# Third and fourth mLSTM output gates and two tiles of the first merge gate as seven-product pairs

## The chip, the cores and the metric

The kernel runs on one core of one Trainium2 chip. The metric is the device time of one execution in microseconds; lower is better. The core has a matrix engine (TensorE, PE in the profile, with its weight loads as PEld), a vector engine (VectorE, DVE), an activation engine (ScalarE, ACT), GpSimd (POOL) and SyncE (SP). The last two and ACT also issue DMAs. Matrix products are summed in eight PSUM banks; everything else lies in SBUF or in DRAM.

## What is computed

Two layers of a hybrid encoder block on one sequence of 512 frames, model width 1024, in float32. What matters of the reference:

```python
h = rmsnorm(x, norm1_g[i])
z = h @ w_in[i] + b_in[i]
_, _, mv, mo, mi, mf, rq, rk, rv, rg, gm, gr = split_cols(z)
...
hm = mlstm_chunkwise(q, k, v, log_i, log_f)          # 4 heads, dk = dv = 256
y_m = sigmoid(mo) * head_layernorm(hm, m_norm_g[i], M_HEADS)
...
merged = sigmoid(gm) * (y_m @ w_bm[i]) + sigmoid(gr) * (y_r @ w_br[i])
x = x + merged @ w_out[i]
```

`mo` (1024 columns, 256 per head) are the output gates of the four mLSTM heads, `gm` (1024 columns) is the first merge gate. The change concerns how the columns of `mo` for the third and fourth head, and columns 256 to 511 of `gm`, are multiplied out.

## The kernel before

**Precision.** Each float32 operand is split into a high part that the matrix engine takes as it is and a low part that is the remainder (`split`, L320: one ACT copy, one DVE subtraction). A product is three matmuls, high by high, high by low and low by high (`mm3`, L501).

**Units.** All weights pass through a written-out list of units (`unit_list`, L172), consumed in order. A `T8` unit (`t8`, L506) is one 1024 x 128 tile of weights against all 512 frames: 8 row blocks of 3 matmuls with 512 columns, 24 in all. A `V` unit is a quarter of a value projection. A `PAIR` unit (`run_pair`, L538) is two neighbouring tiles, 256 columns of weights, done as a 2 x 2 block product by a seven-product scheme: the weights are cut into four blocks (B11 to B22), the frames into two halves and the rows of x into even and odd tiles, and seven products P1 to P7 of half the size take the place of eight. Each is 4 x 3 matmuls with 256 columns, 84 in all. A `WIDE` unit is the same scheme on 1024 columns of weights.

**What a pair needs besides.** Sums of weight blocks: t1 and t3 are made once in DRAM by accumulating DMAs on GpSimd's queue (`step`, L372, L379); t2 and t4 are formed on DVE when the pieces are prepared (L481, L484). A pair has four pieces: A is B11 and t1, C is B22 and t3, B is B21 and t2, D is t4 (L97). Sums of the operand: `xs_sums(k)` (L1264) adds the high and low part of two tiles of the normed x, forms four combinations of their halves and splits them again, k = 0 to 3 for the eight tiles. The products P5, P6, P3 and P7 read these sums; P1, P2 and P4 read x itself. `pair_tiles` (L618) gathers the seven results into two 128 x 512 outputs: four ACT copies, three DVE additions, each of 256 columns, and calls `consume` when P4 has been added. P4 is put off: it is issued when the next unit, or the next scores or attention, calls `flush` (L529). One of the two outputs comes with its sign turned, which `SIGN` (L62) undoes.

**Preparation.** Raw pieces are loaded by SyncE's queue in the order of use into four buffers, and a fifth while there is room (`fill_raws`, L415), and split into three shared buffers and one for D (`prep_next`, L445), for single tiles two units ahead (`LOOK`), for pairs by the table `READY` (L122). The load of a block sum waits for its DMAs.

**Pace of the sums.** Each unit adds to a credit what the constants say of its time and its loads (`tick`, L387): a share (`SHARE` until the unit of layer 0's third retention gate, `LATER` from there) of 5.45 us for a tile less 1.5 for its load, 9.9 and 3.9 for a pair. At credit 0 or more the next sum step goes out (`pace`, L383) and takes off `STEP`. The steps run over the groups in the order of `groups()` (L148), layer 0 first, and each waits for the matmul last issued. A load asserts that the steps of its block were issued.

**Order of the work.** The build lays out each engine's instructions from priorities that follow the source order and from when it expects their operands; `ahead()` raises the priority of the evictions of pairs. So the order on an engine can differ from the source's.

**The mLSTM stage (L1331 to L1384).** In layer 0 it lasts from about 7 to 284 us. Head by head: projections q and k (four `T8`) with a causal convolution on DVE; `m_scores(h)`, the decayed score matrix; `m_attend(h)`, the numerators, whose head norm (`head_stats`, `head_scale` L880) runs on DVE with a power on GpSimd; `m_gates(h)`, two `T8` with a sigmoid on ACT; `m_back(h)`, eight transposes of the scaled numerators, multiplied by the gates on DVE. Two value projections lie in between (`mv_vals`). `xn_tile(k)` makes the normed x. Until all eight are there, the products run on the un-normed operand `xa`, and their results are multiplied by the norm on DVE (L894). The first four tiles of `gm` are `T8` units as well (`gm_tile`, L1249): two ahead of the scores of head 0, the third between the gates and the transposes of head 0, the fourth between the gates and the transposes of head 2. They are spilled to DRAM on ACT's queue and read back for the merge (`bm_tile`, L1391). The last four tiles of `gm` are pairs already (`gm_gates`, L1241). The stage ends with `rv_vals(0)`, the first `WIDE` unit.

Of the kernel before, what the change touches and what calls it, by code (L numbers as in the profile page):

```python
# [108 lines left out]
HALVES = [(WIDE[x][0], u) for x, u in TURNS]  # L109

SOON = ("w_in", 0, CGM + 2 * P)
STEP, SHARE, LATER = 1.13, 0.75, 0.75
TIME = {"PAIR": (9.9, 3.9), "WIDE": (5.45, 2.7), "FULL": (9.9, 5.0)}


# [32 lines left out]
def groups():  # L148


    g = {}
    for i in range(L):
        def rqk(h):
            return [("w_in", 0, c + k * 256) for k in (h, h + 1) for c in (CRQ, CRK)]

        g[i, "rv0"] = [("w_in", 0, CRV)]
        g[i, "rqk0"] = rqk(0)
        g[i, "gm"] = [("w_in", 0, CGM + 256 * p) for p in (2, 3)]
        g[i, "rw0"] = [("w_in", 0, CRG)]
        g[i, "rv2"] = [("w_in", 0, CRV + 1024)]  # L160
        g[i, "rqk2"] = rqk(2)
        g[i, "rw2"] = [("w_in", 0, CRG + 1024)]
        g[i, "gr"] = [("w_in", 0, CGR + 256 * p) for p in range(4)]
        for b in range(4):
            f = [p for c, p in FPAIRS[i] if c == b]
            if f:
                g[i, f"fp{b}"] = [("w_ff1", 0, b * 1024 + 256 * p) for p in f]
            g[i, f"ff{b}"] = [("w_ff2", b * 1024, 256 * p) for p in range(4)]
    return g


def unit_list(i):  # L172
# [19 lines left out]
    def mo(h):  # L192
        for d in range(2):
            t8("w_in", CO + h * 256 + d * P)
# [5 lines left out]
    def full(w, col=0, row=0, lo=0, hi=8):  # L200
        for c in range(lo, hi):
            t8(w, col + c * P, row)
# [3 lines left out]
    full("w_in", CGM, 0, 0, 2)  # L206
    mqk(1)
    mo(0)
    full("w_in", CGM, 0, 2, 3)
    mqk(2)  # L210
    mo(1)
    v(CV + 512)
    mqk(3)
    mo(2)
    full("w_in", CGM, 0, 3, 4)
    mo(3)
    u.append(("WIDE", (i, "rv0"), 0))
    full("w_bm", 0, 0, 0, 4)
    rqk(0)
# [34 lines left out]
def build(ctx, tc, ins, out):  # L254
# [755 lines left out]
    for i in range(L):  # L1010
# [125 lines left out]
        def m_gates(h, act, nrm):  # L1136
            return [gated(f"l{i}m{h}o{v}", t8(act, f"l{i}m{h}o{v}"), nrm, AF.Sigmoid, bcol(i, "bo", 2 * h + v))
                    for v in range(2)]

        def m_back(h, gs, num):  # L1140
            gate_out(f"l{i}m{h}o", gs, num, [bcol(i, "gmn", 2 * h + v) for v in range(2)], ym, 2 * h)

# [98 lines left out]
        def gm_gates(p):  # L1241
            def consume(g):
                for d in range(2):
                    ac.activation(g[d], g[d], AF.Sigmoid, bias=bcol(i, "bgm", 2 * p + d), scale=SIGN[d])
                    gm[2 * p + d] = g[d]

            pair_tiles(f"l{i}bgm{p}", xs, consume)

        def gm_tile(c, act, nrm):  # L1249

            g = gated(f"l{i}bgm{c}", t8(act, f"l{i}bgm{c}"), nrm, AF.Sigmoid, bcol(i, "bgm", c))
            nc.scalar.dma_start(gm_dram[i, c], g)
# [5 lines left out]
        def xn_tile(k, x=x):  # L1258
            t = tmp(f"l{i}xnr{k}")
            ve.scalar_tensor_tensor(t, x[k], n1.col(k), n1.b, OP.mult, OP.mult)  # L1260
            xn[0][k] = bpool.tile([P, T], F32R, name=f"l{i}xnh{k}", tag="big", bufs=KT)
            split(t, xn[0][k], xn[1][k])
# [91 lines left out]
        qk = m_qk(1, xa, n1, xn_tile)  # L1354
        num = m_attend(0, pt, vv)
        gs = m_gates(0, xa, n1)
        xn_tile(4)
        gm_tile(2, xa, n1)
        for k in (5, 6, 7):
            xn_tile(k)  # L1360
        m_back(0, gs, num)
        xa_pool.release()
# [5 lines left out]
        xs_sums(0)  # L1368
        num = m_attend(1, pt, vv)
        gs = m_gates(1, xn, None)  # L1370
        vv = mv_vals(1, xn, None, lambda: m_back(1, gs, num))
        xs_sums(1)
        pt = m_scores(2, qk)
        qk = m_qk(3, xn, None)
        xs_sums(2)
        num = m_attend(2, pt, vv)
        gs = m_gates(2, xn, None)
        gm_tile(3, xn, None)
        m_back(2, gs, num)
        xs_sums(3)  # L1380
        pt = m_scores(3, qk)
        gs = m_gates(3, xn, None)
        num = m_attend(3, pt, vv)
        vv = rv_vals(0, lambda: m_back(3, gs, num))  # L1384

# [453 lines left out]
```

## Time and profile before

| | |
|---|---|
| median of 3 runs | 2285.81 us (2283.84 to 2286.82) |
| the profiled execution | 2280.56 us |
| its span, first to last instruction | 2278.8 us |
| TensorE busy | 2261.4 us, 99% of the span |
| VectorE busy | 1746.8 us, 77% |
| ScalarE busy | 1280.9 us, 56% |
| GpSimd busy | 605.8 us, 27% |
| moved by DMA | 499.32 MB |

Times in the trace are counted from the span's start. Names are the program's own with buffer numbers left out: `l0m2o` is layer 0, mLSTM head 2 (the third, counted from 0), output gate; `l0bgm` a single tile of the first merge gate, `l0bgm2` its pair 2 with the banks a, b and c behind the name; `l0m1s` head 1's scores, `l0m0ot` head 0's transposes, `l0m2z` head 2's projections, `l0xsl` the low part of the sums of normed x; `w` the split weights of a single tile, `w_A` to `w_D` those of a pair. A row of the view in order of time gives start, duration, engine, line, operation and operands, with the engine's idle time ahead of it and what ended that in square brackets; a matmul's duration includes the fill and drain, so the rate is read from one start to the next. A row of the grouped view ends with the count, the busy time, the mean duration in ns, and the idle time ahead. A row of the view by stretch gives its ends, its length and the busy time of each engine.

### The profile page before, as it was taken

How to read it: one execution, taken by the hardware profiler on the slowest of the kernel's cores; microseconds unless marked ns; L12 is line 12 of the kernel's file. 1: busy time of each engine (PE TensorE's matmuls, PEld its weight loads, DVE VectorE, ACT ScalarE, POOL GpSimd, SP SyncE). 2: the span in 40 equal slices, each digit the busy share in tenths (PEclk: the TensorE clock that was granted, in tenths of full speed). 3: DMA queues.
4: the chain of work that ended last, by engine and by line, in shares of the span. 5: the costliest groups of instructions: out<-in, count | busy, mean ns of one | idle time of the engine just before them, and what ended most of it. 6: DMA issues, size and time to landing. Idle time of an engine off the chain costs nothing.

```text
span 2278.8 us, 36395 instructions
## 1 busy us (share of the span) xinstructions
PE 2261.4 (99%) x13532; PEld 2007.0 (88%) x13532; DVE 1746.8 (77%) x2680; ACT 1280.9 (56%) x1881; POOL 605.8 (27%) x952
## 2 busy tenths in 40 slices
PE   9999999999999999999999999999999999999998
PEld 7888899888898899999888888998888988999997
DVE  7877777887676877787779687678867678887786
ACT  6766544554554556556557564455545546576564
POOL 3332222223124322223432322221231243111112
PEclk9999999999999999999999999999999999999999
DMA  6776887787879888888887768877877898888841
GB/s 213 183 196 175 246 227 220 220 234 213 244 218 277 217 229 229 242 240 223 228 222 194 186 180 242 240 210 218 240 217 218 249 266 215 258 233 231 251 161 61
DMA packets 185889, 499.32 MB, mean 219 GB/s; under 512 B 26400, under 2 KB 26784, under 8 KB 185712
## 3 DMA queue, kind: packets, MB, share of 16 engines
q0 software_dynamic: 57520, 188.53, 37.1%
q1 hardware_dynamic: 112208, 280.04, 36.5%
q10 hardware_dynamic: 15984, 28.44, 3.6%
q8 instruction: 106, 1.74, 0.3%
q14 instruction: 71, 0.58, 0.1%
HBM read 478.03 MB, written 194.51 MB: 295 GB/s over the span
## 4 chain that ended last, share of the span: by engine, by line
PE 92%; DVE 4%; ACT 1%; DMA 1%; issue 1%; POOL 0%; DVEq 0%; ACTq 0%; SPq 0%; POOLq 0%
PE l0f L502 2%; PE l0f L503 2%; PE l0f L504 2%; PE l0br L502 1%; PE l1br L502 1%; PE l1br L503 1%; PE l0br L503 1%; PE l1br L504 1%; PE l0br L504 1%; PE l1f L502 1%; PE l1f L503 1%; PE l1f L504 1%; DVE w_B L322 1%; PE l0pg L502 1%; PE l1bm L503 1%
## 5 line engine op out<-in xcount | busy, mean ns | idle before, releaser
L322 DVE TENSOR_TENSOR w<-wr,w 128x1024 fp32r<-128x1024 f32 (+1 forms) x193 | 233.9, 1215 | 47.8 <-ACT w L321 47.0
L321 ACT ACTIVATE w<-wr 128x1024 fp32r<-128x1024 f32 (+1 forms) x193 | 199.7, 1041 | 120.4 <-issue 28.4
L321 ACT ACTIVATE w_B<-wr 128x1024 fp32r<-128x1024 f32 x123 | 130.5, 1061 | 149.3 <-PE l0bm L504 13.1
L322 DVE TENSOR_TENSOR w_B<-wr,w_B 128x1024 fp32r<-128x1024 f32 x123 | 150.0, 1221 | 52.9 <-ACT w_B L321 52.3
L321 ACT ACTIVATE w_C<-wr 128x1024 fp32r<-128x1024 f32 x75 | 79.3, 1058 | 64.4 <-DMA wr<-wpairs 10.4
L322 DVE TENSOR_TENSOR w_C<-wr,w_C 128x1024 fp32r<-128x1024 f32 x75 | 93.2, 1243 | 28.4 <-ACT w_C L321 24.6
L322 DVE TENSOR_TENSOR w_A<-wr,w_A 128x1024 fp32r<-128x1024 f32 x75 | 91.6, 1221 | 14.8 <-ACT w_A L321 14.6
L321 ACT ACTIVATE w_A<-wr 128x1024 fp32r<-128x1024 f32 x75 | 79.0, 1053 | 38.5 <-DMA wr<-wpairs 8.8
L321 ACT ACTIVATE w_t<-wr 128x1024 fp32r<-128x1024 f32 x56 | 59.4, 1060 | 61.6 <-PE l1g2va L610 6.3
L322 DVE TENSOR_TENSOR w_t<-wr,w_t 128x1024 fp32r<-128x1024 f32 x56 | 68.1, 1220 | 21.3 <-ACT w_t L321 20.7
L321 ACT ACTIVATE w_D<-wr 128x512 fp32r<-128x512 f32 x75 | 47.3, 631 | 65.1 <-DVE wr L484 17.5
L502 PE MATMUL l0f<-l0n2h,w 128*128 128x512 f32 x176 | 68.7, 390 | 0.0
L503 PE MATMUL l0f<-l0n2l,w 128*128 128x512 f32 x176 | 68.6, 390 | 0.0
L504 PE MATMUL l0f<-l0n2h,w 128*128 128x512 f32 x176 | 68.5, 389 | 0.0
L322 DVE TENSOR_TENSOR w_D<-wr,w_D 128x512 fp32r<-128x512 f32 x75 | 51.6, 688 | 14.5 <-ACT w_D L321 14.1
L379 POOL DMA_DIRECT2D s30t<-wpairs x24 | 16.8, 701 | 89.8 <-PE l1o20a L559 8.7
L504 PEld LDWEIGHTS l0f<-l0n2h,w 128*128 128x128 f32 x176 | 33.0, 188 | 7.0
L502 PEld LDWEIGHTS l0f<-l0n2h,w 128*128 128x128 f32 x176 | 33.0, 188 | 6.6
L503 PEld LDWEIGHTS l0f<-l0n2l,w 128*128 128x128 f32 x176 | 33.0, 188 | 6.4
L502 PE MATMUL l1f<-l1n2h,w 128*128 128x512 f32 x96 | 37.6, 391 | 0.0
L503 PE MATMUL l1f<-l1n2l,w 128*128 128x512 f32 x96 | 37.4, 390 | 0.0
L504 PE MATMUL l1f<-l1n2h,w 128*128 128x512 f32 x96 | 37.4, 389 | 0.0
(5828 smaller groups left out, 9067.1 us busy)
## 6 DMA issues: line engine op xcount, KB each, us to landing
wr<-wstream SPq DMA_DIRECT2D x189, 512.0 KB, 4.9
wr<-wpairs SPq DMA_DIRECT2D x225, 256.0 KB, 4.1
wr<-wwide SPq DMA_DIRECT2D x48, 512.0 KB, 4.6
s3t<-wwide POOLq DMA_DIRECT2D x24, 256.0 KB, 4.9
s6t<-wwide POOLq DMA_DIRECT2D x24, 256.0 KB, 5.3
s18t<-wwide POOLq DMA_DIRECT2D x24, 256.0 KB, 5.7
s21t<-wwide POOLq DMA_DIRECT2D x24, 256.0 KB, 5.4
s24t<-wpairs POOLq DMA_DIRECT2D x24, 256.0 KB, 6.0
```

The costliest lines, as they stand in the source:

```text
L321: a = ac.activation(hi_ap, src, AF.Copy)
L322: return a, ve.tensor_sub(lo_ap, src, hi_ap.bitcast(F32))
L379: dma = gp.dma_start(piece(g, x, p, q), piece(g, MADE[x][a], p, q), max_dma_last_dim=4096, **kw)
L502: te.matmul(o, sh, mh, start=first, stop=False)
L503: te.matmul(o, sh, ml, start=False, stop=False)
L504: cur["mm"] = te.matmul(o, sl, mh, start=False, stop=last)
```

## The change

The output gates of heads 2 and 3 and tiles 2 and 3 of `gm` become one group `mo` of three pairs per layer: the gates of head 2, the two tiles of `gm`, the gates of head 3. The group stands first in `groups()`, so its sums come first in each layer. The third `gm` tile leaves its place in head 0. `xs_sums(1)`, `(2)` and `(3)` stand one place sooner, so that all are written ahead of the first of the pairs. `m_gates_pair` gives back a list that is filled when P4 is done; `gm_spilled` spills both tiles when their pair is done. `SHARE` goes from 0.75 to 0.83. The planner then has 269 units and 694 sum steps, before it had 275 and 670.

```diff
-STEP, SHARE, LATER = 1.13, 0.75, 0.75
+STEP, SHARE, LATER = 1.13, 0.83, 0.75
...
+        g[i, "mo"] = [("w_in", 0, CO + 512), ("w_in", 0, CGM + 256), ("w_in", 0, CO + 768)]
         g[i, "rv0"] = [("w_in", 0, CRV)]
...
     full("w_in", CGM, 0, 0, 2)
     mqk(1)
     mo(0)
-    full("w_in", CGM, 0, 2, 3)
     mqk(2)
     mo(1)
     v(CV + 512)
     mqk(3)
-    mo(2)
-    full("w_in", CGM, 0, 3, 4)
-    mo(3)
+    for p in range(3):
+        pair("mo", p)
     u.append(("WIDE", (i, "rv0"), 0))
...
+        def m_gates_pair(h):
+            gs = []
+
+            def consume(g):
+                for d in range(2):
+                    ac.activation(g[d], g[d], AF.Sigmoid, bias=bcol(i, "bo", 2 * h + d), scale=SIGN[d])
+                gs.extend(g)
+
+            pair_tiles(f"l{i}m{h}o", xs, consume)
+            return gs
...
+        def gm_spilled(p):
+            def consume(g):
+                for d in range(2):
+                    ac.activation(g[d], g[d], AF.Sigmoid, bias=bcol(i, "bgm", 2 * p + d), scale=SIGN[d])
+                    nc.scalar.dma_start(gm_dram[i, 2 * p + d], g[d])
 
             pair_tiles(f"l{i}bgm{p}", xs, consume)
...
         num = m_attend(0, pt, vv)
         gs = m_gates(0, xa, n1)
-        xn_tile(4)
-        gm_tile(2, xa, n1)
-        for k in (5, 6, 7):
+        for k in (4, 5, 6, 7):
             xn_tile(k)
         m_back(0, gs, num)
...
         xs_sums(0)
         num = m_attend(1, pt, vv)
         gs = m_gates(1, xn, None)
+        xs_sums(1)
         vv = mv_vals(1, xn, None, lambda: m_back(1, gs, num))
-        xs_sums(1)
+        xs_sums(2)
         pt = m_scores(2, qk)
         qk = m_qk(3, xn, None)
-        xs_sums(2)
+        xs_sums(3)
         num = m_attend(2, pt, vv)
-        gs = m_gates(2, xn, None)
-        gm_tile(3, xn, None)
+        gs = m_gates_pair(2)
+        gm_spilled(1)
         m_back(2, gs, num)
-        xs_sums(3)
         pt = m_scores(3, qk)
-        gs = m_gates(3, xn, None)
+        gs = m_gates_pair(3)
         num = m_attend(3, pt, vv)
         vv = rv_vals(0, lambda: m_back(3, gs, num))
```

More of the change, by code (lines that the diff above doesn't have):

```diff
@@ L1245, in consume @@
                     gm[2 * p + d] = g[d]
+            pair_tiles(f"l{i}bgm{p}", xs, consume)
+        def gm_spilled(p):
[3 more added lines that the diff above has]
+                    nc.scalar.dma_start(gm_dram[i, 2 * p + d], g[d])
             pair_tiles(f"l{i}bgm{p}", xs, consume)
```

## The prediction

> **What bounds the kernel now.** I read the page first, then the matrix engine's own rows in order of time, then the busy time by stretch, then the vector engine's rows at the two places where the change moves matrix work.
>
> ```profile
> span 2278.8 us, 36395 instructions
> ...
> PE 2261.4 (99%) x13532; PEld 2007.0 (88%) x13532; DVE 1746.8 (77%) x2680; ACT 1280.9 (56%) x1881; POOL 605.8 (27%) x952
> ...
> PE 92%; DVE 4%; ACT 1%; DMA 1%; issue 1%; POOL 0%; DVEq 0%; ACTq 0%; SPq 0%; POOLq 0%
> ```
>
> TensorE (PE) is busy for 99% of the span and makes 92% of the chain that ended last. So time goes only where matrix work goes, or where PE is made to wait. VectorE (DVE) is second at 77%, but that is an average; the stages that the change touches are fuller:
>
> ```profile
> 95.60:142.40 46.80, 46.80 (x233) 39.81 (x233) 44.24 (x83) 33.88 (x57) 14.80 (x23) 1.00 0.68 175
> 156.80:179.50 22.70, 22.70 (x106) 18.87 (x105) 9.37 (x11) 7.17 (x9) 6.02 (x9) 1.00 0.79 213
> 205.30:244.70 39.40, 39.40 (x214) 34.30 (x214) 29.50 (x64) 25.77 (x48) 10.43 (x19) 1.00 0.71 196
> 244.70:283.70 39.00, 39.00 (x178) 32.40 (x177) 32.51 (x49) 17.05 (x19) 9.99 (x15) 1.00 0.84 259
> 283.70:323.20 39.50, 39.50 (x254) 35.74 (x253) 24.61 (x33) 15.69 (x22) 10.51 (x16) 1.00 0.89 239
> ```
>
> These are stretches of layer 0: length, then busy time of PE, weight loads, DVE, ScalarE (ACT) and GpSimd, the clock, the DMA share. In the first, DVE works 44.24 of 46.80 us; PE never waits there, but has little cover.
>
> **The gain: fewer columns.** Six one-tile products per layer become three pairs. Both kinds of unit are in the trace:
>
> ```profile
> 208.94 0.40 PE L502 MATMUL l0m2o<-l0xnh,w 128*128 128x512 f32 x1
> ...
> 219.85 0.39 PE L502 MATMUL l0bgm<-l0xnh,w 128*128 128x512 f32 x1
> ...
> 654.12 0.28 PE L557 MATMUL l0gr1a<-l0xnh,w_A 128*128 128x256 f32 x1
> ...
> 662.31 0.40 PE L502 MATMUL l0br<-l0yr1h,w 128*128 128x512 f32 x1
> ```
>
> Two tiles (48 matmuls of 512 columns) take 219.85 - 208.94 = 10.91 us. The first 72 matmuls of a pair (256 columns) take 662.31 - 654.12 = 8.19 us, 114 ns each; all 84 take 9.56. A pair saves 1.35 us, a layer 4.05, both layers **8.1 us**. The numbers of matmuls elsewhere do not change.
>
> The Trainium skill ("TensorE: Matmul & The Clock Gate", section Back-to-back issue gap) gives a rule against this: in a stream of weight loads and matmuls the spacing is set by both, 81 ns for 128 columns and 131 ns for 512. A straight line between them gives an estimated 98 ns for 256, so 8.2 us for a pair against 6.3 for two tiles, and 11.7 us lost over six pairs. The trace disagrees: 227 ns for 512 columns, and half of that for 256.
>
> **What it adds, on DVE and ACT.**
>
> ```profile
> L322 DVE TENSOR_TENSOR w_A<-wr,w_A 128x1024 fp32r<-128x1024 f32 x75 | 91.6, 1221 | 14.8 <-ACT w_A L321 14.6
> L484 DVE TENSOR_TENSOR wr<-wr 128x512 f32<-128x512 f32 x49 | 33.8, 689 | 1.0
> L637 DVE TENSOR_TENSOR l0r0brqy<-l0r0brqb,l0r0brqy 128x256 f32<-128x256 f32 x1 | 0.4, 418 | 0.0
> ```
>
> A pair makes DVE split pieces A, B and C (3 x 1.22), split D (half as wide, like the second row, 0.69), form t2 and t4 (2 x 0.69) and add three quarter outputs (3 x 0.42): 7.0 us, where two tiles cost two splits as wide as the first row, 2.4. That is 4.6 us more per pair, 13.7 per layer; the third gate tile's multiply by the norm (about 0.7) goes. ACT gains about as many splits and has 25.77 of 39.40 us in use there: nothing on the path. One group of sums of normed x (two 512-wide adds, four 256-wide, two 512-wide splits: about 4 x 0.69 + 4 x 0.42 = 4.4 us) leaves the stretches 205-284 because each is now a place sooner: the one that used to run at 182-188 can fill the empty 156-180, where DVE is busy for 9.37 of 22.70 us. So 205-284 goes from 62.0 us of DVE work to 71.3, in 78.4 - 4.05 = 74.4 us of PE: 96% full. It fits, but what is late stays late.
>
> **Place 1: the third gate tile leaves the first head.** Its 5.4 us stood between head 0's output gates and head 0's transposes (l0m0ot), which need the heads' scaled numerators.
>
> ```profile
> 109.53 0.67 DVE L322 TENSOR_TENSOR l0m1kl<-l0m13cv,l0m1kh 128x512 fp32r<-128x512 f32 x1
> 113.03 1.38 DVE L882 TENSOR_SCALAR l0m0num<-l0m0num,l0m0mv,l0m0hv 128x256 f32<-128x256 f32 x4 [0.96 <-POOL l0m0hv L1132]
> 121.17 1.28 DVE L322 TENSOR_TENSOR l0xnl<-l0xnr,l0xnh 128x512 fp32r<-128x512 f32 x2
> ```
> ```profile
> 110.14 0.39 PE L502 MATMUL l0bgm<-l0n1h,w 128*128 128x512 f32 x1
> ...
> 115.58 1.03 PE L888 MATMUL l0m0ot<-ident,l0m0num 128*128 128x128 f32 x8
> 116.37 0.48 PE L1097 MATMUL l0m1rp<-l0grr,l0sel 128*128 128x512 f32 x1
> ...
> 120.57 0.40 PE L502 MATMUL l0m2z<-l0xnh,w 128*128 128x512 f32 x1
> ```
>
> Today PE reaches the transposes at 115.58, 1.2 us after the scaling ended (114.41). After the change it is there at 110.14, 4.3 us early. Head 1's scores (116.37 to 120.57, 4.2 us) are ready from 110.20 and could be run first. If they are, little is lost; if not, 4.3 us is. Between these ends I take **1.1 us**: DVE idled 0.96 us ahead of the scaling with later work at hand, so the order was laid down for a scaling that much sooner, and PE would turn to the transposes that much too soon. Head 2 then starts at 110.14 + (120.57 - 115.58) + 1.1 = 116.2 and wants the last normed x in its last eighth, 4.8 us later; DVE has it at 122.45 today, 1.9 sooner without the gate's multiply and one split: just in time.
>
> **Place 2: the first pair.** Its product P5 needs the last sums of normed x, and P6 needs piece B. DVE today at the same places in the source, with the sums one index lower:
>
> ```profile
> 211.92 0.67 DVE L322 TENSOR_TENSOR l0m3kl<-l0m33cv,l0m3kh 128x512 fp32r<-128x512 f32 x1
> ...
> 214.66 0.67 DVE L322 TENSOR_TENSOR l0xsl<-l0xs2u,l0xsh 128x512 fp32r<-128x512 f32 x1
> ...
> 215.72 1.20 DVE L322 TENSOR_TENSOR w<-wr,w 128x1024 fp32r<-128x1024 f32 x1
> ```
>
> PE wants P6 at 208.94 + 24 x 0.114 = 211.7; B's split, in the place of this last one, ends at 216.9: 5.3 us late. Head 3's scores (4.2 us) are ready from 212.6 and can stand in. Ends: 5.3 and, with P3 (1.4 us) run ahead too, near 0.6; I take 5.3 - 4.2 = **1.1**.
>
> That PE's order does bend around what is late, the trace shows:
>
> ```profile
> 901.21 0.38 PE L557 MATMUL l0o11a<-l0hh,w_A 128*128 128x256 f32 x1
> ...
> 902.37 0.39 PE L557 MATMUL l0o10c<-l0hh,w_C 128*128 128x256 f32 x1 [0.43 <-DVE l0x L1558]
> ```
>
> The next unit's product (o11) stands ahead of o10's own third one, which waited for DVE.
>
> **The other pairs.** Where a pair follows busy DVE work, B is late by a little:
>
> ```profile
> 327.37 0.28 PE L558 MATMUL l0bgm2a<-l0xsl,w_B 128*128 128x256 f32 x1
> 327.96 0.39 PE L559 MATMUL l0bgm2a<-l0xsh,w_B 128*128 128x256 f32 x1 [0.31 <-DVE w_B L322]
> ```
>
> 0.59 instead of 0.11: **0.5 us** a layer, between 0 and 1.5 (each of three).
>
> **Transfers.** Twelve more sum steps a layer go first on GpSimd's queue, ahead of all the others; the pace of the sums in the first part of layer 0 rises from 0.75 to 0.83 of the time, so the steps come 17% faster (2.68 instead of 2.29 per tile). By the planner's constants (a credit of -12 at the start, 0.83 x 5.45 - 1.5 = 3.02 a tile, 1.13 a step) the new group's twelve steps of layer 0 are out after (12 + 13.6) / 3.02 = 8.5 units; their first load comes about five units ahead of their unit 31, so no load waits for them. What it costs is DMA time: the share of 0.89 at 283-323 rises by at most the 0.08 of the constant. I cost it at nothing: the loads are cut off from PE by four buffers. If that cover goes, see the rival. The spill of the third gate tile moves later on ACT's queue and is read back later still, by the merge: nothing.
>
> **The sum.** Per layer -4.05 + 1.1 + 1.1 + 0.5 = -1.35; both layers -2.7 us. The profiled execution took 2280.56 us (span 2278.8), the median of the runs is 2285.81, 5.25 more; I carry the difference over: 2285.8 - 2.7 = **2283.1 us**.
>
> **The rivals.**
>
> *All of it is hidden* (chance 0.27): PE is refilled at both places and DVE keeps up. Only half of the 0.5 remains per layer: -7.6, 2278.2 us. For it: DVE idles at 157-179 and the pairs of the trace mostly run at full rate. Against: 96% in 205-284.
>
> *PE waits in source order* (0.14), the case on the other side: neither place is refilled, 4.3 + 5.3 + 0.5 = 10.1 per layer against 4.05: +12.1, 2297.9 us; place 1 alone +3.7, place 2 alone +5.7. The change is slower from the point where a layer's waits pass 4.05 us. For it: place 1 is 4.3 us late by the trace itself. Against: the o11 row.
>
> *The faster sums crowd out the loads* (0.07): if B came 1.6 us later in the six pairs of layer 0 between 305 and 390, that is 9.6 us, less the 2.7: +6.9, 2292.7 us. Against: nothing on PE waits for a DMA today at a share of 0.89.
>
> *Narrow products run slower here* (0.02), the skill's rule. By rows: a weight load
>
> ```profile
> L504 PEld LDWEIGHTS l0f<-l0n2h,w 128*128 128x128 f32 x176 | 33.0, 188 | 7.0
> ```
>
> of 188 ns that nothing hid would make a pair 15.8 us, 4.9 more than two tiles, +29 in all. The row of 114 ns speaks against it.
>
> **How the numbers follow.** My forecast has 0.50, spread by about 2 us around -2.7. A measurement of this kernel can tell about 0.2%, 4.6 us, from no change. Faster by more: 0.26 of the hidden case and 0.08 of the forecast, 0.34. Slower by more: 0.12 of the source-order case (the rest is place 1 alone), 0.06 of the crowding, 0.02 of the narrow products and 0.01 of the forecast, 0.21. Within: 0.45. The range goes from the whole gain with nothing lost (2277.7) to place 2 alone unfilled (2291.5). That leaves out both places unfilled (about 0.09), most of the crowding and the narrow products (0.06) and some noise below.
>
> **What would show it.** Right: six 72-matmul pair stretches of about 8.2 us; l0m1s ahead of l0m0ot and l0m3s inside the first pair; waits on w_B or the last xs there of about 1 us a layer. Wrong: waits of 4 us or more at l0m0ot or at the first P6 (source order); DMA named before w_A to w_C on PE's side in layer 0 (crowding); no such waits and a span near 2271 (all hidden).

## The result, and the profile after

The changed kernel takes 2296.59 us in the median of its five runs, the kernel before 2285.81. One of the five, 4050.86 us at a granted clock of 0.71, stands apart; the other four (2297.52, 2291.18, 2294.14 and 2296.59) have their median at 2295.4. The ratio on record is **1.0048** (95%: 1.0035 to 1.0062), and 2295.4 to 2285.81 is 1.0042: slower by 10 to 11 us, where I forecast 2283.1 and a range up to 2291.5. The profiled execution is the one of 2297.52 us. The heads of its page, to be read beside those of before:

```profile
span 2295.8 us, 36993 instructions
...
PE 2268.3 (99%) x13748; PEld 2017.3 (88%) x13748; DVE 1772.4 (77%) x2720; ACT 1300.1 (57%) x1917; POOL 620.0 (27%) x976
...
PE 39%; DVE 5%; ACT 2%; issue 1%; DMA 1%; POOL 0%; DVEq 0%; SPq 0%; POOLq 0%; ACTq 0%
```

The span is 17.0 us longer, though the count of matmuls is as the plan says (216 more, narrower ones). PE is still "99% busy": 17 us is less than the rounding of such a share. The chain's shares add up to 48% only, so it was lost halfway and can't be set against the 92% of before. What tells is the list of PE's waits (us in total, times, longest):

```profile
PE l0m0ot L887 <- DVE l0m0num L881: 2.0, 1, 2.0
PE l1m0vp L829 <- DVE l1m00z L1063: 2.0, 1, 2.0
...
PE l1bgm1a L558 <- DVE w_A L321: 0.8, 1, 0.8
PE l0bgm1a L558 <- DVE w_A L321: 0.8, 1, 0.8
PE l0m2oc L556 <- ACT l0m2oy L634: 0.8, 1, 0.8
PE l1m2oc L556 <- ACT l1m2oy L634: 0.8, 1, 0.8
PE l1bgm L503 <- DVE w L321: 0.7, 1, 0.7
PE l0r0brqa L556 <- DVE l0r0brqy L642: 0.6, 1, 0.6
```

Short waits, each below what the prediction named as a sign of trouble (4 us), but at the two places that it named, in both layers, and at one that it did not (`l1m0vp`, the first value projection of layer 1). No DMA is among them; one stands a step behind the last (below).

To find the cost I measured each stage on PE from the start of its first matmul to the start of the next stage, and compared it with "ideal": the length before less the columns that the change took out of that stage. Place 1 runs from `l0m0o` (99.23 before, 97.21 after) to `l0m2z` (120.57 and 116.95), place 2 from `l0m2a` (205.35 and 201.72) to `l0bm` (283.72 and 287.61).

| stage | before | ideal | after | lost |
|---|---|---|---|---|
| place 1, layer 0 | 21.33 | 15.89 | 19.74 | 3.85 |
| place 1, layer 1 | 21.33 | 15.89 | 16.97 | 1.08 |
| place 2, layer 0 | 78.37 | 79.77 | 85.89 | 6.12 |
| place 2, layer 1 | 78.62 | 80.02 | 86.31 | 6.29 |
| start of layer 1, `l1m0vp` to `l1m1z` | 37.90 | 37.90 | 41.22 | 3.32 |
| rotated key of retention head 0, layer 0 | 9.52 | 9.52 | 10.50 | 1.0 |

("Ideal" moves one tile from place 1 to place 2, where three pairs then take 4.05 less than six tiles: 21.33 - 5.44, and 78.37 + 5.45 - 4.05.) Lost in all 21.7. Gained: 8.1 by six pairs, and 2.0 that the start of the program happened to be shorter. A further 5.9 is a slower step of narrow matmuls all over the program, which varies from run to run (last section). 21.7 - 8.1 - 2.0 + 5.9 = 17.5, where the spans say 17.0.

At the rotated key PE waits for an addition on DVE, and that addition stands in DVE's order behind a sum of weight blocks that waits for its load. That row on DVE, before and then after:

```profile
314.86 0.69 DVE L481 TENSOR_TENSOR wr<-wr,wr 128x512 f32<-128x512 f32 x1 [1.02 <-DMA wr<-wpairs]
```
```profile
319.96 0.69 DVE L480 TENSOR_TENSOR wr<-wr,wr 128x512 f32<-128x512 f32 x1 [2.23 <-DMA wr<-wpairs]
```

The load is asked for 4.7 us after the start of the rotated query in both kernels; after the change it is there 1.2 us later. In layer 0 this wait is 1.0 to 1.6 us in the three kernels with the pace at 0.75 (before, e2, e12), and 2.1 to 3.7 in the fifteen with 0.83 whose profile puts it down to a load, e1 and e5 without a new pair among them. In the 12 us from the start of the rotated query seven steps of the sums go out instead of six, their queue moves 1.47 MB instead of 1.09, and such a load (`wr` from `wpairs`) takes 5.8 us from issue to landing instead of 4.5.

### The profile page after: what moved, and what is told of

It reads as the page before. It is cut to its first block, busy times and chain, and to the rows that moved or that the text cites. A ratio compares the mean times of both kernels' runs of the same rounds, so it can differ in the third digit from the quotient of the medians.

```text
span 2295.8 us, 36993 instructions
## 1 busy us (share of the span) xinstructions
PE 2268.3 (99%) x13748; PEld 2017.3 (88%) x13748; DVE 1772.4 (77%) x2720; ACT 1300.1 (57%) x1917; POOL 620.0 (27%) x976
## 5 line engine op out<-in xcount | busy, mean ns | idle before, releaser
L320 ACT ACTIVATE w<-wr 128x1024 fp32r<-128x1024 f32 (+1 forms) x181 | 187.2, 1042 | 122.9 <-issue 29.2
L321 DVE TENSOR_TENSOR w<-wr,w 128x1024 fp32r<-128x1024 f32 (+1 forms) x181 | 219.4, 1214 | 35.0 <-ACT w L320 31.6
L320 ACT ACTIVATE w_B<-wr 128x1024 fp32r<-128x1024 f32 x129 | 136.8, 1061 | 154.3 <-PE l0bm L503 13.1
L321 DVE TENSOR_TENSOR w_B<-wr,w_B 128x1024 fp32r<-128x1024 f32 x129 | 157.3, 1221 | 53.1 <-ACT w_B L320 52.7
L320 ACT ACTIVATE w_C<-wr 128x1024 fp32r<-128x1024 f32 x81 | 85.6, 1057 | 63.2 <-issue 8.2
L321 DVE TENSOR_TENSOR w_C<-wr,w_C 128x1024 fp32r<-128x1024 f32 x81 | 99.7, 1231 | 26.9 <-ACT w_C L320 26.6
L321 DVE TENSOR_TENSOR w_A<-wr,w_A 128x1024 fp32r<-128x1024 f32 x81 | 98.9, 1221 | 16.8 <-ACT w_A L320 14.1
L378 POOL DMA_DIRECT2D s32t<-wpairs x24 | 16.8, 699 | 87.9 <-PE l1o10a L558 9.0
L483 DVE TENSOR_TENSOR wr<-wr 128x512 f32<-128x512 f32 x55 | 37.9, 688 | 1.0
L501 PE MATMUL l1f<-l1n2h,w 128*128 128x512 f32 x96 | 37.6, 391 | 0.0
```

The source lines that it names most:

```text
L320: a = ac.activation(hi_ap, src, AF.Copy)
L321: return a, ve.tensor_sub(lo_ap, src, hi_ap.bitcast(F32))
L378: dma = gp.dma_start(piece(g, x, p, q), piece(g, MADE[x][a], p, q), max_dma_last_dim=4096, **kw)
L483: ve.tensor_tensor(r[:, :Q], r[:, :Q], r[:, Q:], OP.add)
L501: te.matmul(o, sh, mh, start=first, stop=False)
```

## Place 1 in the rows

PE in order of time, after:

```profile
107.89 0.39 PE L503 MATMUL l0m0o<-l0n1h,w 128*128 128x512 f32 x1
110.32 0.66 PE L887 MATMUL l0m0ot<-ident,l0m0num 128*128 128x128 f32 x2 [2.04 <-DVE l0m0num L881]
110.64 0.78 PE L1096 MATMUL l0m1rp<-l0grr,l0sel 128*128 128x512 f32 x1
...
111.92 0.78 PE L501 MATMUL l0m1s<-l0m1qh,l0m1kh 128*128 128x512 f32 x1
```

PE ends the output gates and goes straight to the transposes, 2.04 us too soon. Head 1's scores stand behind them, not ahead. Then the second loss: the rows that follow are twice as long as those of before (0.78 instead of 0.39). The busy time by stretch, with the granted clock as the third number from the end, says why:

```profile
107.00:110.30 3.30, 1.28 (x6) 0.74 (x5) 2.37 (x6) 1.97 (x2) 1.25 (x2) 1.00 0.71 154
110.30:113.50 3.20, 3.18 (x12) 2.74 (x13) 3.20 (x7) 2.28 (x4) 0.00 (x0) 0.50 0.32 113
113.50:117.00 3.50, 3.50 (x24) 3.28 (x23) 3.50 (x7) 3.41 (x6) 0.00 (x0) 0.97 0.35 137
```

After the wait the clock was 0.50 for 3.2 us, which costs 1.6 us more. The Trainium skill ("TensorE: Matmul & The Clock Gate", section Part 1: The HAM clock gate) says that PE falls to half its clock after an idle window of about 3.4 us and comes back after a busy one of that length, and that the window runs free. The half and the length agree; but here 2.04 us of idleness were enough, and in an experiment below they were not.

## Place 2 in the rows

The first pair on PE (from 205.31), its rows that waited:

```profile
208.67 0.38 PE L556 MATMUL l0m2oc<-l0xsh,w_A 128*128 128x256 f32 x1 [0.56 <-ACT l0xsh L320]
...
209.95 0.38 PE L557 MATMUL l0m2oc<-l0xsl,w_A 128*128 128x256 f32 x1 [0.50 <-DVE l0xsl L321]
...
211.22 0.39 PE L556 MATMUL l0m2oc<-l0xsh,w_C 128*128 128x256 f32 x1 [0.77 <-ACT l0m2oy L634]
...
213.35 0.39 PE L558 MATMUL l0m2oa<-l0xsh,w_B 128*128 128x256 f32 x1 [0.47 <-DVE w_B L321]
...
218.40 0.39 PE L558 MATMUL l0bgm1a<-l0xnh,w_A 128*128 128x256 f32 x1 [0.77 <-DVE w_A L321]
```

And DVE in the same time:

```profile
206.60 0.68 DVE L1285 TENSOR_TENSOR l0xsr<-l0xnh,l0xnl 128x512 f32<-128x512 f32 x1
...
209.22 0.68 DVE L321 TENSOR_TENSOR l0xsl<-l0xs3u,l0xsh 128x512 fp32r<-128x512 f32 x1
...
211.03 0.67 DVE L321 TENSOR_TENSOR l0xsl<-l0xs3u,l0xsh 128x512 fp32r<-128x512 f32 x1
...
212.09 1.20 DVE L321 TENSOR_TENSOR w_B<-wr,w_B 128x1024 fp32r<-128x1024 f32 x1
...
215.23 1.38 DVE L881 TENSOR_SCALAR l0m2num<-l0m2num,l0m2mv,l0m2hv 128x256 f32<-128x256 f32 x4 [1.21 <-POOL l0m2hv L1131]
216.53 0.68 DVE L321 TENSOR_TENSOR w_D<-wr,w_D 128x512 fp32r<-128x512 f32 x1
217.13 1.22 DVE L321 TENSOR_TENSOR w_A<-wr,w_A 128x1024 fp32r<-128x1024 f32 x1
```

Everything the pair needs comes a little late, one after the other: the last sums of normed x are still being made while their product P5 runs, P5's bank is then evicted late, B comes behind the sums, and A of the second pair stands behind the head norm of head 2, for which DVE *idled* 1.21 us waiting for GpSimd. Five idle times of 3.07 us on PE; each also costs the overlap of the matmul before it (207.84 to 208.67 is 0.83 from start to start, 0.11 in a stream), so the pair's 84 matmuls take 14.17 instead of 9.56. The two pairs behind it take 9.71 and 9.70. The first pair is thus 4.6 of the 6.1 us; 0.7 more lie at head 3's products (`l0m3a`, 4.30 instead of 3.56) and 0.4 at the `WIDE` unit (38.63 instead of 38.20).

The stretches of after and before:

```profile
201.72:244.00 42.28, 39.21 (x304) 37.02 (x303) 35.61 (x76) 30.38 (x59) 10.45 (x18) 1.00 0.69 178
244.00:287.61 43.61, 43.61 (x221) 36.65 (x221) 34.41 (x50) 21.45 (x25) 11.49 (x19) 1.00 0.91 285
```
```profile
205.35:283.72 78.37, 78.37 (x390) 66.69 (x389) 61.97 (x112) 42.78 (x66) 20.41 (x34) 1.00 0.78 228
```

DVE's work went from 61.97 to 35.61 + 34.41 = 70.02 us, close to the 71.3 that I had worked out, but I spread it over the whole stretch: the half with the pairs had it full, the other half had room.

## The experiments

The theory from these rows: **two places lose, because what PE would need to be refilled with is behind it in its order, and the work of the first pair comes late from DVE and ACT.** Rivals: DVE is simply too full (then moving work about doesn't help), the moved sums, or the faster pace of the sums. All ratios are against the kernel before on the same chip, with 95% intervals; "lost" is against the stage's ideal.

### The parts alone

**e1_sums_only**: the kernel before, with the pace 0.83 and the sums a place sooner.

```diff
-STEP, SHARE, LATER = 1.13, 0.75, 0.75
+STEP, SHARE, LATER = 1.13, 0.83, 0.75
...
+        xs_sums(1)
         vv = mv_vals(1, xn, None, lambda: m_back(1, gs, num))
-        xs_sums(1)
+        xs_sums(2)
         pt = m_scores(2, qk)
         qk = m_qk(3, xn, None)
-        xs_sums(2)
+        xs_sums(3)
...
-        xs_sums(3)
```

> The kernel before with SHARE at 0.83 and the three groups of sums of normed x a place sooner; no pairs, no tile moved. Theory of places (the time was lost where a pair or a move makes PE wait: the transposes of head 0, the first pair, the start of layer 1): nothing is lost here, within 3 us of before (2283 to 2289). Rival 1 (the faster sums crowd the loads, or the sooner sums of normed x press on VectorE): 5 to 10 us slower, with PE waiting for w, w_A to w_C in layer 0.

1.0031 (1.0020 to 1.0041). Place 2 went from 78.37 to 80.75, and to 81.18 in layer 1, with none of the new pairs in it. The row that waits is in the first `WIDE` unit:

```profile
254.94 0.50 PE L609 MATMUL l0r0vc<-w_t,l0xsh 128*128 128x512 f32 x1 [2.06 <-DVE w_t L322]
```

**e5_share_only**: the kernel before with the pace 0.83 (the first line of the diff above).

> The kernel before with SHARE at 0.83 alone. The run with the sums of normed x sooner as well was 0.31% (about 7 us) slower than before. If the sooner sums of normed x did that (its waits, on w_t in both retention value stages and on a rotated query, stand in both layers, while SHARE acts in layer 0 alone): within 2 us of before. If the pace of the block sums on GpSimd's queue did it: 5 to 7 us slower, most of it in layer 0.

1.0008 (0.9999 to 1.0016): about nothing. Of the 2.4 and 2.6 us that e1 lost in place 2, this kernel has 0 and 1.1. Its profiled execution, 3.6 us above the median of its runs, loses 3.7 us at the rotated key of layer 0 (13.25 instead of 9.52): DVE waits 3.66 us there for the load. So the sums' place costs some 4 us by the stages, and 0.23%, some 5, by the ratios.

**e12_sums_early_alone**: the kernel before, with all three groups of sums behind the gates of head 1, so one, two and three places sooner.

```diff
         gs = m_gates(1, xn, None)
+        for k in (1, 2, 3):
+            xs_sums(k)
         vv = mv_vals(1, xn, None, lambda: m_back(1, gs, num))
-        xs_sums(1)
...
-        xs_sums(2)
...
-        xs_sums(3)
```

> The kernel before with all sums of normed x from the second group on behind head 1's gates; nothing else. The sums one place sooner, with the faster pace, were 0.31% over before, of which the pace alone made 0.08%. If the place counts (VectorE's order near the retention values): within 0.1% of before. If any earlier sums cost: 0.2% over before again.

1.0007 (0.9998 to 1.0016); place 2 is 78.37 in both layers. The sums aren't dear; one place sooner, at the faster pace, is just a bad place for them.

**e2_move_only**: the kernel before, the third gate tile moved as it is from head 0 to beside the fourth.

```diff
         gs = m_gates(0, xa, n1)
-        xn_tile(4)
-        gm_tile(2, xa, n1)
-        for k in (5, 6, 7):
+        for k in (4, 5, 6, 7):
             xn_tile(k)
...
         gs = m_gates(2, xn, None)
+        gm_tile(2, xn, None)
         gm_tile(3, xn, None)
```

> The kernel before with the third gate tile moved from head 0 to a place beside the fourth in head 2, both as single tiles; no pairs. Theory of places: the wait at the transposes of head 0 comes back as in the changed kernel, 3.8 us in layer 0 and 1.1 in layer 1, so +5 us over before (0.2%), and nothing at the start of layer 1. Rival 2 (only pairs cost, by their work on VectorE and ScalarE): no difference from before.

1.0031 (1.0020 to 1.0043). Place 2 is 83.84: longer by 5.47, the moved tile, and nothing else is lost there. Place 1 loses 2.26 in layer 0 and 2.92 in layer 1:

```profile
PE l1m0ot L887 <- DVE l1m0num L881: 2.7, 1, 2.7
PE l0m0ot L887 <- DVE l0m0num L881: 2.0, 1, 2.0
```

So the loss of place 1 belongs to the move alone, pairs or not.

**e4_two_pairs_no_move**: the change with its two gate tiles of `gm` back as single tiles where they were; two pairs a layer.

```diff
-        g[i, "mo"] = [("w_in", 0, CO + 512), ("w_in", 0, CGM + 256), ("w_in", 0, CO + 768)]
+        g[i, "mo"] = [("w_in", 0, CO + 512), ("w_in", 0, CO + 768)]
...
+        xn_tile(4)
+        gm_tile(2, xa, n1)
-        for k in (4, 5, 6, 7):
+        for k in (5, 6, 7):
...
         gs = m_gates_pair(2)
-        gm_spilled(1)
+        gm_tile(3, xn, None)
```

> The changed kernel with the third and fourth gate tile as single tiles at their old places; the pairs are the gates of heads 2 and 3. Theory of places: no wait at the transposes of head 0; at the first pair P5, P6 and P3 still wait, 3.5 to 4.5 us a layer, while the wait for the next pair's piece A goes; two pairs gain 2.7 a layer. Sum: +1 to +2 us a layer, 2287 to 2290. Rival 2 (work on VectorE decides, a third less of it here): the waits at the first pair shrink to under 2 us, and the kernel is faster than before by 1 to 3 us.

1.0051 (1.0038 to 1.0065). Place 1 is whole again (21.33 in both layers) and so is the start of layer 1 (37.90), yet place 2 loses 8.2 and 5.2 over its ideal. So the pairs at this spot lose without the moved tile. The sums are still a place sooner here; e11 below takes that away and 3.7 and 2.3 are left.

### Trying to refill PE

**e3_scores_first**: head 3's scores ahead of the first pair, which is what the prediction said "can stand in".

```diff
         num = m_attend(2, pt, vv)
+        pt = m_scores(3, qk)
         gs = m_gates_pair(2)
         gm_spilled(1)
         m_back(2, gs, num)
-        pt = m_scores(3, qk)
```

> The changed kernel with head 3's scores (about 4 us of PE work that waits for nothing by 209 us) ahead of the first pair in the source. Theory of places: the first pair's products P5, P6 and P3 start some 4 us later, and of the 6.2 us lost there per layer 3 to 4 go: 6 to 8 us less than the changed kernel, 2289 to 2291. Rival 2 (VectorE as a whole is too full between 205 and 284 us): the waits only move to later products, within 2 us of the changed kernel.

1.0114 (1.0101 to 1.0128), the worst of all; place 2 is 92.92 and 90.52. ACT and DVE:

```profile
218.26 0.63 ACT L320 ACTIVATE l0m3ph<-l0m3p 128x512 fp32r<-128x512 f32 x1 [4.17 <-DVE l0m3p L854]
...
219.88 1.04 ACT L320 ACTIVATE w_A<-wr 128x1024 fp32r<-128x1024 f32 x1
```
```profile
216.25 1.38 DVE L881 TENSOR_SCALAR l0m2num<-l0m2num,l0m2mv,l0m2hv 128x256 f32<-128x256 f32 x4 [1.88 <-POOL l0m2hv L1131]
217.55 0.68 DVE L854 TENSOR_TENSOR l0m3p<-l0m3s,l0m3D 128x512 f32<-128x512 f32 x1
```

The scores bring work of their own. ACT's copy of their first rows waits 4.17 us for a product on DVE, which stands behind the scaling of head 2 and so behind GpSimd; the copy of A stands behind it on ACT, and PE waited 5.1 us for that piece in each layer. Filling PE's gap put a longer chain ahead of the pieces.

**e7_sums_early**: the change with all three groups of sums behind the gates of head 1, as in e12.

> The changed kernel with all sums of normed x from the second group on written right behind head 1's gates, where VectorE has idle time, so that none is left near the first pair. If the first pair is held up by the last sums (waits on l0xsh, l0xsl and, behind them, on the eviction of P5): 1.5 to 3 us a layer less than the changed kernel, about 0.25% over before. If what counts is that piece B and the next piece A are prepared late behind head 2's norm: within 2 us of the changed kernel, with the wait only moved on to w_B.

1.0032 (1.0021 to 1.0042) against 1.0048; place 2 is 82.89 and 83.51, the loss there 3.1 and 3.5 instead of 6.1 and 6.3. The first pair takes 9.80; in layer 0 one wait of that stretch is left from the list above:

```profile
214.59 0.39 PE L558 MATMUL l0bgm1a<-l0xnh,w_A 128*128 128x256 f32 x1 [0.76 <-DVE w_A L321]
```

The stage's gain is clear; by the whole times the two intervals overlap.

**e8_pieces_first**: the change, with the splits of the three pairs' pieces raised in priority.

```diff
-            in_order("prep", *split(r[:, :w], *out_))
+            with tc.high_priority(AHEAD if units[n][0] == "PAIR" and units[n][1][1] == "mo" else 0):
+                in_order("prep", *split(r[:, :w], *out_))
```

> The changed kernel with a raised priority for splitting the pieces of the three new pairs, so that they do not stand behind head 2's norm in ScalarE's and VectorE's order. If late pieces hold PE at the first pairs: the waits on w_B and on the second pair's w_A go (0.5 and 0.8 us), 1 to 2 us a layer less than the changed kernel, about 0.3 to 0.4% over before. If VectorE is too full there: what is pushed back is late in its place (the sums of normed x, head 2's scaling at the transposes m2ot), and the time stays within 2 us or grows.

1.0074 (1.0061 to 1.0086): worse. The pieces come, and what they passed is late, the sums (1.1 us of waiting in each layer) and head 3's scaled scores:

```profile
238.88 0.39 PE L502 MATMUL l0m3a<-l0m1vh,l0m3ph 128*128 128x258 f32 x1 [1.50 <-ACT l0m3ph L320]
```

**e6_hole_filled**: the change, with the second gate tile of `gm` moved from ahead of head 0's scores into the hole that the third left.

```diff
-        for c in range(2):
-            gm_tile(c, xa, n1)
+        gm_tile(0, xa, n1)
...
-        for k in (4, 5, 6, 7):
+        xn_tile(4)
+        gm_tile(1, xa, n1)
+        for k in (5, 6, 7):
             xn_tile(k)
```

> The changed kernel with the second gate tile moved from ahead of head 0's scores to the place that the third one left, between gates and transposes of head 0. If the wait at the transposes is what the move cost (moving alone was 0.31%, about 7 us): 5 us less than the changed kernel, about 0.26% over before. If the tile only was cover that is now missing ahead of the scores: the same as the changed kernel, with new waits before l0m0s and l1m0s.

1.0047 (1.0034 to 1.0061), as the change itself. The wait at `m0ot` is gone, but the tile is missed where it was: 1.2 us on its own weights in place 1, and the start of layer 1 loses 4.7 instead of 3.3. A hole was moved, not filled.

### The rest of the loss

**e9_start_held**: e7, and the raised priority that the weights of the first value projection have in layer 0 in layer 1 too.

> The changed kernel with all sums of normed x behind head 1's gates (as the run that was 0.32% over before), and with the priority that layer 0's first value projection has for splitting its weights given to layer 1's as well. If the 3 us that layer 1's start lost are the one late split in ScalarE's order (wait of 2.0 us in l1m0vp, 0.9 at l1bgm): 3 us less, about 0.18% over before. If that split was late because its weights were: the wait stays, 0.32%.

1.0037 (1.0024 to 1.0049). `l1m0vp` still waits 2.0 us; the weights were not the cause of that. The start of layer 1 is 1.0 us shorter than in e7 (40.28), as the wait at `l1bgm` is gone.

**e10_scores_ahead** is e9 with head 1's scores written ahead of head 0's transposes, which takes nothing from elsewhere.

```diff
             xn_tile(k)
+        pt = m_scores(1, qk)
         m_back(0, gs, num)
...
-        pt = m_scores(1, qk)
```

> The run with layer 1's start held, and with head 1's scores ahead of head 0's transposes in the source. If PE only lacked work between gates and transposes: the wait of 2.0 us at l0m0ot and the switches go, 4 to 4.5 us less over both layers, within 0.05% of before. If the scores' masks push head 0's scaling and the last normed x back on VectorE (as head 3's scores did to the first pair's pieces): new waits at l0m0ot or l0m2z, and no gain over the run with the start held.

Place 1 is 15.78 in both layers: nothing is lost there. That is the refill that I had counted on; it comes when the source says so. The ratio, 1.0032 (1.0019 to 1.0044), doesn't show it, because the start of layer 1 grew to 41.85.

**e13_banks_kept**: the change, with a counter of results set on. `ps()` gives every eighth result a bank apart, in turn; three pairs for six tiles ask for fewer results, and all results behind them move in the round. Layer 1's first value projection then wants a bank in which a projection of head 0 still waits for DVE.

```diff
         gs = m_gates(0, xa, n1)
+        cur["turn"] += 1
...
         gs = m_gates_pair(3)
+        cur["turn"] += 4
```

> The changed kernel with the counter of PSUM banks set on by one where the third gate tile left and by four behind the third pair, so that every later product takes the bank it took before. If the loss at layer 1's start (the fourth bank of the value projection is still held by a projection that VectorE evicts late: 2.0 us in l1m0vp, 0.9 at l1bgm) comes from the number of banks that pairs take: those waits go, 3 us less than the changed kernel, 0.35% over before. If it comes from how the weights are prepared: no change.

The start of layer 1 is 37.90, as before: the count was the cause of those 3.3 us. But the total is no better, 1.0058 (1.0046 to 1.0071). Now PE comes sooner to the next hole, place 1 of layer 1, and that loses 4.1 instead of 1.1:

```profile
PE l1m0ot L887 <- DVE l1m0num L881: 2.3, 1, 2.3
PE l0m0ot L887 <- DVE l0m0num L881: 2.0, 1, 2.0
```
```profile
111.00:114.00 3.00, 3.00 (x18) 2.67 (x19) 3.00 (x6) 1.96 (x4) 0.00 (x0) 1.00 0.19 68
1250.00:1252.00 2.00, 2.00 (x11) 1.77 (x11) 2.00 (x6) 1.28 (x3) 0.00 (x0) 0.60 1.01 297
1252.00:1256.00 4.00, 4.00 (x21) 3.57 (x21) 4.00 (x7) 3.79 (x7) 0.00 (x0) 0.77 0.16 64
```

Here the clock stayed at 1.00 after the wait in layer 0 and fell after that in layer 1: a wait of 2 us may cost its clock or not.

**e15_scores_ahead_banks_kept**: sums early, scores ahead and the counter kept (e7, e10's edit and e13's).

> Banks kept, all sums of normed x behind head 1's gates, head 1's scores ahead of head 0's transposes. Without the banks kept it was 0.32% over before, with 3.9 us lost at layer 1's start. If these three (sums, hole, banks) are all but the pairs' own waits: 0.12 to 0.18% over before, the rest at the first pairs. If something else costs as much: 0.3% again.

1.0016 (1.0007 to 1.0025), the best with three pairs, but still slower. Place 1 loses nothing, the start of layer 1 0.2. Of PE's waits at the places of the change there remain:

```profile
PE l1m2z L502 <- DVE l1xnl L321: 1.3, 1, 1.3
...
PE l0bgm1a L558 <- DVE w_A L321: 0.8, 1, 0.8
...
PE l1bgm1a L558 <- DVE w_A L321: 0.8, 1, 0.8
PE l0m2z L502 <- DVE l0xnl L321: 0.5, 1, 0.5
```

Place 2 still loses 2.8 and 3.4, and with place 1 gone PE runs up against the last normed x, 1.8. That is 8.2 lost, and 1.1 at the rotated key make it 9.3, against 8.1 gained. This profile's span is 7.4 us longer than that of before, and most of that lies elsewhere: 5.3 us of slower steps (last section), and its longest wait, 2.0 us at `l1o20c`, far behind the change. Which of these make up the 0.16% of the whole runs is not shown.

**e14_pieces_first_sums_early** (sums early, counter and e8's priority) and **e16_all_four** (the scores ahead as well) ask whether the priority helps once the sums are out of the way.

> Banks kept, all sums of normed x behind head 1's gates, and the pieces of the three pairs split with raised priority. Raised priority alone made the changed kernel 0.26% slower, with the last sums late. If pieces were late only because they stand behind head 2's norm and the sums: with the sums gone the wait on the second pair's w_A (1.1 us a layer) goes, 2 us less than the same without the priority, about 0.1% over before. If VectorE and ScalarE are too full at the pairs: the head's products m3a wait instead (2 us and more a layer, as with the priority alone), 0.25% or more over before.

> The run before this one and the pieces' raised priority too. If the queue theory holds: within 0.1% of before, at best 0.1% under. If the pairs are too much for VectorE and ScalarE in this place: 0.2% or more over before, with waits at m3a.

1.0041 (1.0028 to 1.0053) and 1.0032 (1.0019 to 1.0045). No: place 2 is 84.0 and 85.0 in layer 0 where e15 has 82.58; `m3a` waits 1.5 or more for head 3's scores in both, as in e8. The first pair of e14 in layer 0 takes 9.55, so its pieces do come in time; the loss has only moved from the pairs to the head behind them.

**e11_two_pairs_sums_early**: e4 with the sums early.

> The kernel with two pairs (gates of heads 2 and 3) and the third and fourth gate tile as single tiles at their old places, with all sums of normed x behind head 1's gates. It was 0.51% over before with the sums at the places of the change. If sums and pairs compete for VectorE at the first pair, and the move is what else costs: the gain of 5.4 us stands against about 1.7 us a layer of small waits, 0 to 0.15% under before. If pairs cost by their own work on VectorE and ScalarE: 0.2% or more over before.

1.0025 (1.0016 to 1.0033). Lost in place 2: 3.7 and 2.3, and in layer 1 1.0 at place 1 and 1.4 at the rotated key; gained by four pairs 5.4.

### Pairs where there is room

**e17_one_pair_late**: the kernel before with one pair a layer more: tiles 2 and 3 of `gm` as the first of the late gate pairs, behind the retention's first key, and in head 0's hole a gate tile of head 1 (on un-normed x, spilled and fetched); pace 0.83, counter kept.

```diff
-        g[i, "gm"] = [("w_in", 0, CGM + 256 * p) for p in (2, 3)]
+        g[i, "gm"] = [("w_in", 0, CGM + 256 * p) for p in (1, 2, 3)]
...
-        gm_tile(2, xa, n1)
+        m_spilled(1, (0,), 2)
...
-        gm_tile(3, xn, None)
...
-        for p in (2, 3):
+        for p in (1, 2, 3):
```

> The kernel before with one new pair a layer in another place: the third and fourth gate tile as a pair among the merge's first products, behind the rotated query and key of the first retention head (SHARE 0.83). The hole in head 0 is filled by the first gate tile of head 1 (multiplied by the norm, spilled, read back), nothing fills head 2's, the banks are kept. If pairs lose only where VectorE and ScalarE are full and PE is near the operand: 1.35 us a layer gained, 0.4 lost at m2ot, so 0.08 to 0.12% under before. If new pairs lose their gain anywhere: 0 to 0.1% over.

0.9998 (0.9989 to 1.0007). Place 1 is 21.33 in both layers, place 2 in layer 0 shorter by 5.44, the tile that left. In layer 1 the `WIDE` unit waits:

```profile
PE l1r0va L608 <- DVE w_t L321: 1.2, 1, 1.2
```

Its 168 matmuls take 40.21 instead of 38.45. 2.7 are gained, 1.8 given back there, and 0.9 at the rotated key of layer 0 (10.41), where DVE waits 2.35 us for the load.

**e18_two_pairs_late**: all four early gate tiles of `gm` as two late pairs; the gates of heads 0 and 1 fill the holes, spilled and fetched.

> The same with all four early gate tiles as two pairs a layer in the late place, no gate tile left in the heads: head 0's gates ahead of its scores, head 1's gates and scores between head 0's products and its transposes (both heads' gates spilled and read back). Gain 5.4 us in all; waits of about 0.4 at m0ot, 1.2 at m2z and 0.4 at m2ot a layer: 0.05 to 0.1% under before. If the cover is thinner than that (head 1's transposes 10.9 us sooner, head 0's gates read back late): 0.1% and more over.

1.0058 (1.0044 to 1.0071). Now PE waits in head 1 (2.3 us for weights at `l1m1vp`, 1.1 twice at `l0m1vp`). None of these versions beats the kernel before by more than its interval.

## Why the prediction was wrong

**The gain** was right. The pairs that nothing disturbs take what the sum says: 9.71 and 9.70 for the second and third in layer 0, against the 9.56 of the prediction's row, no more than the slower step of this run (below) makes of it. -8.1 us stands.

**Place 1** failed by the step "Head 1's scores (116.37 to 120.57, 4.2 us) are ready from 110.20 and could be run first", priced at 1.1. They weren't run first. The scaling did come sooner, some 2 us after the gates (110.32) and not 4.3, as I had half foreseen; but PE stood and waited, and the price was 3.85 in layer 0 (2.04 of waiting, 1.6 by the halved clock) and 1.08 in layer 1, or 4.1 there when the start of the layer did not hide it (e13). e10 and e15 show that the refill is possible, only not that the build finds it.

**Place 2** failed by "Head 3's scores (4.2 us) are ready from 212.6 and can stand in", also priced at 1.1; the stage cost 6.1 and 6.3, and the first pair alone 4.6. The scores stayed behind both pairs, and e3, which puts them in front, costs far more. I priced one late item, B. B was 0.47 late; the larger part are the sums, P5's eviction and the next A, a chain of small delays. The error was to take two engines' work as independent: what refills PE loads DVE and ACT.

The evidence for both was the o11 row, the build turning around a late operand. It showed that the order *can* bend, at another place and with expectations that need not hold here. It should have had less weight.

**The sums' move** was costed as a relief ("leaves the stretches 205-284"). Alone with the pace it costs 0.31%, without the pace's 0.08% some 4 to 5 us (e1, e5); in e1 that is on the way to the `WIDE` unit's pieces, a place that the prediction doesn't have. In the changed kernel the `WIDE` unit loses only 0.4 us a layer, and the late sums show at the first pair instead: sums early give back 3.0 and 2.8 us there (e7).

**The fullness of DVE** was misread. Its work came out near the sum (70.02 for 71.3), but the 74.4 us of PE that I set it against forget the gate tile that moves into this stage: with it the stage's ideal is 79.8 us, and with the tile's split (1.2) DVE's work 72.5, so 91% and not 96%. The stage had more room than I said, and lost all the same. "It fits, but what is late stays late" was said and then not priced. Two smaller slips at place 2 change little: B's lateness is 5.2 by its own rows, not 5.3, and the lower end of 0.6 does not follow from 5.3, 4.2 and 1.4.

**The start of layer 1** (3.3) was not in the sum at all: the change alters how many results are asked for, and with it which bank a result far behind it gets.

**Transfers** were costed at nothing ("the loads are cut off from PE by four buffers"), and **the other pairs** at 0.5 a layer for a late B; the new pairs behind the first lose 0.1 to 0.3 each (9.70 to 9.81 against 9.56). The 1.0 us lost in layer 0 is of another kind: DVE waits 1.2 us longer for a load, and the addition that PE waits for stands behind it. So a load does reach PE, by way of DVE's order, and the sign that I named (a DMA in PE's own list) could not show it. It is the mechanism of the crowding rival at a small price; that the pace makes it is likely from the waits at the two paces above, and the whole times leave it open (-0.01% to 0.16% in e5); no run takes the faster pace out of the changed kernel.

**The rival** "PE waits in source order" had 2297.9 and the time is 2296.59, and its mechanism, not refilled, holds at both places. Its own prices do not (4.3 and 5.3 a layer); that the total agrees is luck, partly by the bank's 3.3. I gave it 0.14 for the o11 row's sake. The narrow-product rival is out: the rule of the Trainium skill that the prediction cites made two tiles cheaper than a pair by an estimated 1.9 us, and undisturbed pairs are 1.2 us cheaper than the two tiles' 10.91.

What stays open: which part of the 17.0 us between the two profiled executions is chance. The medians differ by 10.8 (9.6 by the four runs), and the profile of before is 5.25 under its own median. Also open is how the 2.8 and 3.4 us that place 2 still loses with the sums early (e15) could go; the priority only moves them.

## What to carry to other kernels

Where PE is the bound, a saving of columns counts only if the engines that prepare its operands have room in that same stretch, in time order and not in the sum; look for the chain of small items that end late one after the other, and follow each wait one step further back than the list shows it. Do not count on a list scheduler to refill PE because it did so once elsewhere: write the refill into the source, and check what that refill asks of the other engines. And when a change alters how many results, tiles or buffers are taken, follow the round they are dealt in to the next stage.

## What the runs showed of the chip

Narrow matmuls (256 columns) keep one step over long stretches, but not always the same one. The same unit, 84 matmuls, from its first row to that of the next unit, before and then after:

```profile
1963.27 0.28 PE L557 MATMUL l1o02a<-l1hh,w_A 128*128 128x256 f32 x1
...
1972.79 0.28 PE L557 MATMUL l1o03a<-l1hh,w_A 128*128 128x256 f32 x1
```
```profile
1979.55 0.28 PE L556 MATMUL l1o02a<-l1hh,w_A 128*128 128x256 f32 x1
...
1989.35 0.28 PE L556 MATMUL l1o03a<-l1hh,w_A 128*128 128x256 f32 x1
```

9.52 and 9.80: 113.3 and 116.7 ns a matmul, at a granted clock of 1.00. A third step of 120.0 ns occurs too. The profile of before has no unit that keeps a slower step throughout (four do for part of it), that of after 18; the difference is 5.9 us. Between the experiments' profiles the sum runs from -0.7 to 5.3 us against that of before. The ten with three pairs have 3.0 on average, the eight others 1.5, and their ranges overlap, so a tie to the pairs is neither shown nor excluded.

Where the step changes, a short wait often stands: in the profile of after it goes from 113 to 117 ns behind a wait of 0.44 us at 2120.29 (`l1o20c`) and stays there for the next 480 matmuls or so. But a wait of 0.43 us of the same unit before the change leaves the step near 114. What decides it was not found; it limits what a single pair of profiles can say to some 5 us.

A wait of about 2 us on PE can halve its clock for about 3 us (place 1 of the change) or leave it at 1.00 (e13, same place), so a wait's price is read from the stage, not from its length.
